# Placing the last two retention steps of each pair of heads with the planner margin that products have

## The chip, the cores and the metric

One Trainium2 chip, one of its cores. The metric is device microseconds (us) of one execution, median of the runs. The engines are TensorE (PE; its weight loads are shown apart as PEld), VectorE (DVE), ScalarE (ACT), GpSimd (POOL) and SyncE (SP, which here only issues DMAs).

## What is computed

One decoder layer over 1024 positions of width 1024, in float32. What matters here is the retention of four heads of 128, done chunk by chunk (8 chunks of 128 positions):

```
scores  = einsum('bhncd,bhnmd->bhncm', qc, kc) * intra_decay
o_intra = einsum('bhncm,bhnme->bhnce', scores, vc)
kv      = einsum('bhnmd,bhnme->nbhde', kc * zeta, vc)
state_n = chunk_decay * state_(n-1) + kv_(n-1)
o       = o_intra + einsum('bhncd,nbhde->bhnce', qc * xi, state)
y_ret   = group_rms_norm(o, ret_norm_g, 4 heads) * silu(rg)
```

Around it stand the other parts of the layer: `u = rms_norm(x)`, a combined projection `u @ w_in` of 3584 columns, a gated causal convolution of 512 channels with a norm of its own, the output projection `w_out`, a squared-ReLU MLP with 4096 hidden units and a last norm.

## The kernel before

**Precision and tiles.** Large products take each float32 operand as the sum of a rounded part and a rest and make three matmuls of 128x512 for each 128x128 block of weights (`mm`, line 403). A weight piece of 128x512 is split by ACT (`wh`, the rounded part) and DVE or POOL (`wl`, the rest), four pieces ahead of its use. Some products are formed in pairs by a seven-product scheme (`pair_in`, products 1, 2, 5, 6, 3, 7, 4) whose right-hand sides t1 to t4 are made by four tasks `rights(j)`, j = 0 to 3, from tiles `xs` loaded again from the input, and stored in tiles `U`.

**Order.** The program order of every engine is fixed when the kernel is built. In the mixer (the first 430 us or so) the large products are written out in a fixed order, and a planner puts the other work between them. The planner has a clock `now`, which advances by SLOT = 2.72 for each slot of 12 large matmuls, and a clock for ACT, DVE and POOL each, which advances by a cost for each instruction issued. For ACT the cost in us is 0.13 + 0.00095 for each column. After each slot `tick` lets the waiting tasks (Python generators) issue what is due. A task that yields an engine gets it when that engine can start within 3.2 us of `now`. A task that yields a number or nothing waits for that margin:

```
want = task.want
if want is None or isinstance(want, float):
    if task.ready + (want or PE_MARGIN) <= now[0] or look > 1e6:
        best = (-1.0, task, None)
        break
```

A task that yields a key waits until another has marked it. `force(key)` issues everything that is waiting, margins or not, until the key is marked. The margins are:

```
SLOT, LOOK, PE_MARGIN, LATE = 2.72, 3.2, 1.2, 0.0
NORM_MARGIN, STEP_MARGIN, POOL_LATE = 6.5, 0.3, 1.0
```

**Retention** (`retention(p, q, k)`, two heads for each p, called pair 0 and pair 1 below) is such a task of ten steps, c = 0 to 9, of which each adds 1.7 to `now`. A step c up to 7 makes the scores of chunk c. A step c from 1 to 8 makes the outputs of chunk c - 1 (lines 625 and 627, and 633 for the state) and normalises them: squares with row sums on ACT, then a chain of small operations on 128x2 numbers `m` (DVE, ACT, three times DVE), then the scaling of the 128x128 outputs on ACT into a tile `on` (tag `h`). A step c from 2 to 9 transposes the `on` of chunk c - 2 on the PE (line 663), and ACT copies the result into the head's tile `q`. So step 8 has four output matmuls and two transposes, and step 9 has two transposes. From step 7 on, the step sets its `ready` to the planner's clock of ACT as it stands after all of its ACT instructions. Step 8 marks ("retention", p). Pair 1 begins behind ("retention", 0), `rights(0)` and `rights(1)` wait for ("retention", 0), `rights(2)` and `rights(3)` for ("retention", 1), and `rights(1)` and `rights(3)` for the t4 of the one before. Step 9 marks the second half of the outputs ("o", h, 1); for heads 2 and 3 a task `put_by` then issues a store of 512 KB to DRAM on SP's queue (line 873), where weight loads (line 162) and loads of `xs` (line 793) are queued too.

Matmuls of pair 1's last steps lie among the products `whole(turn)` for the first five turns of IN_TURNS, at 158 to 233 us of the span; the first `pair_in` follows with the products 1 and 2, then product 5, which is the first to read a t1.

Of the kernel before, what the change touches and what calls it, by code (L numbers as in the profile page):

```python
# [23 lines left out]
NC_ = T // P  # L24
# [17 lines left out]
SLOT, LOOK, PE_MARGIN, LATE = 2.72, 3.2, 1.2, 0.0  # L42
WARM = 10
NORM_MARGIN, STEP_MARGIN, POOL_LATE = 6.5, 0.3, 1.0
# [35 lines left out]
def hybrid_layer(  # L80
# [498 lines left out]
    def retention(p, q, k):  # L579
# [5 lines left out]
        if p:  # L585
            yield "retention", 0
        for c in range(NC_ + 2):
            yield STEP_MARGIN
            now[0] += 1.7
            new = None  # L590
            if c < NC_:
# [165 lines left out]
    for p in range(2):  # L757
        q = rot_tiles(*ropes)
        if p == 0:
            rows_ = norm_rows()  # L760
        k = rot_tiles(*ropes)
        tick()
        spawn(retention(p, q, k), max(clock[dve], clock[pool]))
        retention_task[p] = procs[-1]
        del q, k
# [798 lines left out]
```

## Time and profile before

| what | value |
|---|---|
| median of 3 runs | 1071.01 us (1069.68 to 1071.92) |
| the profiled execution | 1070.03 us |
| its span, first to last instruction | 1068.1 us |
| PE busy | 1054.8 us of the span |
| DVE, ACT, POOL busy | 870.8, 463.6, 561.6 us |
| mean granted clock of TensorE | 0.999 |

The span is what the trace covers; the device time of that execution is 1.9 us longer. Matmuls overlap in the pipeline, so the start of one row to the start of the next is the time that a group takes, and the duration shown is longer. Times within rows are us from the start of the span.

### The profile page before, as it was taken

Reading aid. Unit: us, or ns where it says so; the run is one execution under the profiler, and the core shown is the slowest. Engines: PE = TensorE matmul, PEld = TensorE weight load, DVE = VectorE, ACT = ScalarE, POOL = GpSimd, SP = SyncE. Lnnn points to the kernel's source line nnn. Section 1 sums busy time; section 2 is a strip of 40 time slices with the busy share of each in tenths; the row PEclk is TensorE's granted clock in tenths of the full one; section 3 lists DMA queues with packets and bytes.
Section 4 is the critical chain, followed back from the end, with each engine's and each line's share of the span. In section 5 each row is a group of like instructions: output and inputs, shape, how many; then the busy total and the mean of one; then the engine's idle time right before and its main releaser. Section 6 shows DMA issues by size and latency. Waiting matters only on the chain.

```text
span 1068.1 us, 13853 instructions
## 1 busy us (share of the span) xinstructions
PE 1054.8 (99%) x4860; PEld 879.2 (82%) x4860; DVE 870.8 (82%) x1231; ACT 463.6 (43%) x906; POOL 561.6 (53%) x381
## 2 busy tenths in 40 slices
PE   9999999999999999999999999999999999999997
PEld 8888888788888888788788888888888888888886
DVE  7446546799998665799999989999899899899955
ACT  8211445673437444443343433343443434334453
POOL 6334324367854233559458267277186295384552
PEclk9999999999999999999999999999999999999999
DMA  7121122122223733051221211211301201200204
GB/s 276 65 58 42 38 80 70 63 95 80 69 69 129 256 115 123 11 187 39 61 59 49 79 31 50 90 30 50 99 21 50 89 21 49 90 21 19 69 30 158
DMA packets 39685, 82.25 MB, mean 77 GB/s; under 512 B 4544, under 2 KB 5696, under 8 KB 39616
## 3 DMA queue, kind: packets, MB, share of 16 engines
q1 hardware_dynamic: 39328, 80.85, 23.5%
q8 instruction: 38, 0.62, 0.2%
q10 hardware_dynamic: 288, 0.52, 0.1%
q14 instruction: 31, 0.25, 0.1%
HBM read 71.92 MB, written 9.44 MB: 76 GB/s over the span
## 4 chain that ended last, share of the span: by engine, by line
PE 90%; DVE 6%; ACT 2%; issue 1%; POOL 1%; DVEq 0%; ACTq 0%; POOLq 0%
PE b L403 55%; PE b L1277 23%; PE b L357 4%; PE b L1386 4%; DVE t L74 1%; DVE wl L74 1%; DVE x L74 1%; DVE m L74 1%; ACT h L74 1%; DVE q L74 1%; DVE V L74 1%; PE b L339 0%; PE b L595 0%; PE b L1436 0%; PE b L246 0%
## 5 line engine op out<-in xcount | busy, mean ns | idle before, releaser
L74 ACT CAST wh<-r 128x512 fp32r<-128x512 f32 x286 | 176.6, 620 | 326.4 <-PE b L403 134.4
L403 PE MATMUL b<-U,wh 128*128 128x512 f32 x1024 | 315.8, 390 | 2.0 <-DVE x L74 1.2
L74 DVE TENSOR_TENSOR wl<-r,wh 128x512 fp32r<-128x512 f32 x250 | 232.8, 933 | 89.0 <-ACT wh L74 87.8
L74 POOL TENSOR_TENSOR r<-r,r 128x512 f32<-128x512 f32 x136 | 210.2, 1548 | 114.1 <-DVE wl L74 66.1
L1277 PE MATMUL b<-V,wh 128*128 128x512 f32 x784 | 242.0, 389 | 0.7 <-POOL V L74 0.4
L403 PEld LDWEIGHTS b<-U,wh 128*128 128x128 f32 x1024 | 191.7, 188 | 43.2 <-issue 2.4
L74 DVE TENSOR_TENSOR x<-x,b 128x512 f32<-128x512 f32 (+1 forms) x312 | 195.5, 673 | 28.8 <-PE b L1386 14.3
L403 PE MATMUL b<-U,wl 128*128 128x512 f32 x512 | 199.2, 389 | 0.0
L1277 PEld LDWEIGHTS b<-V,wh 128*128 128x128 f32 x784 | 147.1, 188 | 32.4 <-POOL V L74 0.9
L74 POOL TENSOR_TENSOR t<-t,t 128x512 f32<-128x512 f32 x70 | 106.3, 1523 | 96.4 <-ACT t L74 50.4
L1277 PE MATMUL b<-V,wl 128*128 128x512 f32 x392 | 152.5, 389 | 0.0
L74 POOL TENSOR_TENSOR wl<-r,wh 128x512 fp32r<-128x512 f32 x36 | 51.4, 1432 | 119.3 <-ACT wh L74 116.5
L403 PEld LDWEIGHTS b<-U,wl 128*128 128x128 f32 x512 | 96.1, 188 | 19.9
L403 PE MATMUL b<-uh,wh 128*128 128x512 f32 x304 | 102.3, 396 | 0.0
L403 PE MATMUL b<-ul,wh 128*128 128x512 f32 x304 | 100.5, 390 | 0.0
L403 PE MATMUL b<-uh,wl 128*128 128x512 f32 x304 | 100.2, 389 | 0.0
L1277 PEld LDWEIGHTS b<-V,wl 128*128 128x128 f32 x392 | 73.6, 188 | 15.2
L74 POOL TENSOR_TENSOR V<-t,V 128x512 fp32r<-128x512 f32 x35 | 49.6, 1418 | 67.0 <-ACT V L74 67.0
L74 DVE TENSOR_TENSOR t<-t,b 128x512 f32<-128x512 f32 x112 | 75.8, 677 | 1.7 <-POOL t L74 1.2
L74 ACT ACTIVATE t<-t 128x512 f32<-128x512 f32 x64 | 40.2, 631 | 81.2 <-DVE t L74 80.5
L74 DVE TENSOR_TENSOR V<-t,V 128x512 fp32r<-128x512 f32 x63 | 70.3, 1116 | 0.0
L403 PEld LDWEIGHTS b<-uh,wl 128*128 128x128 f32 x304 | 57.0, 188 | 12.3
(177 smaller groups left out, 1431.3 us busy)
## 6 DMA issues: line engine op xcount, KB each, us to landing
r<-w_up_t SPq DMA_DIRECT2D x64, 256.0 KB, 2.6
r<-w_down_t SPq DMA_DIRECT2D x56, 256.0 KB, 2.7
r<-w_in_t SPq DMA_DIRECT2D x48, 256.0 KB, 2.7
xt<-xT SPq DMA_DIRECT2D x16, 256.0 KB, 5.4
xs<-xT SPq DMA_DIRECT2D x8, 512.0 KB, 5.0
r<-w_out_t SPq DMA_DIRECT2D x16, 256.0 KB, 2.7
x<-xT SPq DMA_DIRECT2D x8, 512.0 KB, 7.9
k<-x SPq DMA_DIRECT2D x6, 512.0 KB, 3.0
```

Of the source, the lines that this page charges most:

```text
L74: return f(out, *args, **kw)
L357: nc.tensor.matmul(vb[i], a[k][:, i * P : (i + 1) * P], b[k // 2][:, vs], start=(k == 0 and a is uh and b is vh), stop=(k == KT - 1 and a ...
L403: nc.tensor.matmul(b, a[:, k, :], rhs(n, k)[r], start=(start and i == 0), stop=(stop and i == len(ops) - 1),)
L1277: nc.tensor.matmul(b, a, r, start=(i == 0), stop=(i == len(ops) - 1))
L1386: nc.tensor.matmul(z, a, b, start=(k == 0 and t == 0), stop=(k == 3 and t == 2))
```

## The change

The steps 8 and 9 of each pair wait for 1.2 us in the planner behind their `ready`, as other tasks with a product in front of them do, instead of 0.3 us. Steps 0 to 7 keep 0.3. No instruction is added or taken away; the instructions of the two steps, and what the planner puts around them, can change place in the engines' program order.

```
@@ -585,7 +585,7 @@
         if p:
             yield "retention", 0
         for c in range(NC_ + 2):
-            yield STEP_MARGIN
+            yield STEP_MARGIN if c < NC_ else PE_MARGIN
             now[0] += 1.7
             new = None
             if c < NC_:
```

## Rows read from the trace of the kernel before

**Rows 1.** The page: the span, and the engines' busy time.

```profile
span 1068.1 us, 13853 instructions
PE 1054.8 (99%) x4860; PEld 879.2 (82%) x4860; DVE 870.8 (82%) x1231; ACT 463.6 (43%) x906; POOL 561.6 (53%) x381
```

**Rows 2.** Waits of PE, whole span: total us, times, longest.

```profile
PE b L663 <- ACT h L74: 2.3, 5, 0.7
```

**Rows 3.** Timeline of PE, pair 0's steps 8 and 9: start, us, [idle before].

```profile
146.83 0.38 PE L625 MATMUL b<-v,h 128*128 128x128 f32 x2
...
147.72 0.49 PE L663 MATMUL b<-ident,h 128*128 128x128 f32 x2
147.97 0.71 PE L403 MATMUL b<-uh,wh 128*128 128x512 f32 x2
...
150.82 0.38 PE L663 MATMUL b<-ident,h 128*128 128x128 f32 x2
150.96 0.71 PE L403 MATMUL b<-uh,wh 128*128 128x512 f32 x2
...
156.51 1.95 PE L339 MATMUL b<-ident,d 128*128 128x128 f32 x16
```

**Rows 4.** Timeline of PE, pair 1's steps 8 and 9.

```profile
204.82 0.38 PE L625 MATMUL b<-v,h 128*128 128x128 f32 x2
...
206.61 0.59 PE L663 MATMUL b<-ident,h 128*128 128x128 f32 x2 [0.73 <-ACT h L74]
206.95 0.71 PE L403 MATMUL b<-uh,wh 128*128 128x512 f32 x2
...
210.32 0.58 PE L663 MATMUL b<-ident,h 128*128 128x128 f32 x2 [0.35 <-ACT h L74]
210.66 0.71 PE L403 MATMUL b<-uh,wh 128*128 128x512 f32 x2
...
216.22 0.62 PE L403 MATMUL b<-uh,wh 128*128 128x512 f32 x2
```

**Rows 5.** Timeline of the other engines, pair 1's steps 7 and 8.

```profile
204.47 1.27 POOL L74 TENSOR_TENSOR xs<-xs 128x512 f32<-128x512 f32 x1
...
204.80 0.96 DVE L74 TENSOR_TENSOR m<-m 128x2 f32<-128x2 f32 x1 [0.27 <-ACT m L74]
...
207.53 0.31 ACT L74 ACTIVATE h<-b 128x128 f32<-128x128 f32 x1
...
207.73 1.30 POOL L74 TENSOR_TENSOR U<-xs,U 128x512 fp32r<-128x512 f32 x1 [1.99 <-ACT U L74]
...
208.21 0.83 DVE L74 SCALAR_TENSOR_TENSOR m<-m,bq 128x2 f32<-128x2 f32 x1 [0.61 <-ACT h L74]
...
209.90 0.62 ACT L74 ACTIVATE h<-b,m 128x128 f32<-128x128 f32 x2 [0.62 <-DVE m L74]
```

**Rows 6.** Timeline of ACT, pair 0's step 8: first square, scaling.

```profile
148.02 0.31 ACT L74 ACTIVATE h<-b 128x128 f32<-128x128 f32 x1
...
149.72 0.63 ACT L74 ACTIVATE h<-b,m 128x128 f32<-128x128 f32 x2 [0.62 <-DVE m L74]
```

**Rows 7.** Timeline of ACT, DVE and PE: the last scaling, t1 of rights(3), product 5.

```profile
226.30 2.18 ACT L74 ACTIVATE xs<-xs,sm 128x1024 f32<-128x1024 f32 x2
...
230.63 0.62 ACT L74 CAST U<-xs 128x512 fp32r<-128x512 f32 x1 [0.40 <-DVE xs L74]
...
234.28 0.68 DVE L74 TENSOR_TENSOR U<-xs,U 128x512 fp32r<-128x512 f32 x1
...
238.89 0.62 PE L403 MATMUL b<-U,wh 128*128 128x512 f32 x2
```

**Rows 8.** Timeline of SP's queue: stores of heads 2 and 3, loads behind them.

```profile
212.59 0.81 SPq L873 DMA_DIRECT2D sp<-q  x2
...
214.31 1.70 SPq L793 DMA_DIRECT2D xs<-xT  x2
```

**Rows 9.** Busy time by stretch: us, PE, PEld, DVE, ACT, POOL, PEclk, DMA share, GB/s.

```profile
211.00:233.40 22.40, 22.40 (x100) 18.54 (x99) 21.32 (x23) 17.03 (x29) 14.25 (x9) 1.00 0.29 106
...
350.00:380.00 30.00, 30.00 (x134) 24.86 (x133) 17.88 (x23) 13.63 (x24) 7.95 (x6) 1.00 0.56 204
```

More of the change, by code (lines that the diff above doesn't have):

```diff
@@ L587, in retention @@
         for c in range(NC_ + 2):
-            yield STEP_MARGIN
+            yield STEP_MARGIN if c < NC_ else PE_MARGIN
             now[0] += 1.7
```

## The prediction, made before the change was run

> **What bounds the kernel now.** I read the page first. PE is busy for 1054.8 of 1068.1 us [rows 1], so a change without arithmetic can only win back the 13.3 us in which PE stands. Next I read who made PE wait. The largest group is the transposes of the retention outputs, line 663, which waited for ACT's scaled tile `on` five times, 2.3 us in all [rows 2]. The change moves four of the ten transposing places, so I then read PE's timeline at these four. In pair 0 neither transpose is shown with a wait [rows 3]. In pair 1 both are: 0.73 us ahead of step 8's and 0.35 us ahead of step 9's [rows 4]. The other three waits lie at steps that the change leaves alone, and make 2.3 - 0.73 - 0.35 = 1.2 us. Last I read the other engines in pair 1 to see why `on` is late [rows 5], and what stands on the end of the two steps: `rights(2)` and `rights(3)`, and the stores [rows 7, 8].
>
> **Does the order change at all?** This follows from the code's own numbers. Step 7 and step 8 issue the same ACT work behind the start of their step: two squares, two scalings, two copies, each 0.13 + 0.00095 x 128 = 0.252, and one small root, 0.132. That is 1.64, so `ready` is at least 1.64 behind the step's `now`. The next `tick` comes 2.72 later. With the old margin 1.64 + 0.3 = 1.94 fits, with up to 0.78 of backlog on ACT to spare, and the rows show it: there is one slot of 12 matmuls between step 8 and step 9 in both pairs [rows 3, 4]. With the new one 1.64 + 1.2 = 2.84 never fits 2.72. So step 8 falls two slots behind step 7, and step 9 two behind step 8, as long as the backlog is under 5.44 - 2.84 = 2.60; for step 8 it is known to be at most 0.78. Step 8 goes one slot later, step 9 two slots later than before. No norm product, which would add 0.43 to `now`, stands between PE's large matmuls there up to the last of [rows 4].
>
> **What is won, place by place.** Starts of rows are used, since durations overlap.
> - Pair 0, step 8: the transposes take 0.49 against 0.38 at step 9 [rows 3], so 0.11 of hidden waiting. The whole step took 147.97 - 146.83 = 1.14, and 1.14 - 0.11 = 1.03 without it.
> - Pair 0, step 9: no wait, nothing won. It goes to the end of the last slot in front of the spreading of the norms at 156.51.
> - Pair 1, step 8: 206.95 - 204.82 = 2.13 [rows 4] against 1.03: 1.10.
> - Pair 1, step 9: from the matmul behind step 8 to the one behind step 9 it is 210.66 - 206.95 = 3.71 against 150.96 - 147.97 = 2.99 in pair 0: 0.72.
>
> Sum: 0.11 + 1.10 + 0.72 = 1.93 us. It exceeds the waits shown, since the matmuls behind a wait start unoverlapped. The slots cut by a step stay as many: PE executes the same instructions, with no added cost. I take the full 1.93, with 0 and 1.93 as the bounds of these three terms.
>
> **Do the waits come back at the new places?** Step 8's transposes need the `on` of chunk 6, which was there by 206.95 at the latest [rows 4]. The new step 8 begins one unbroken slot after 204.82. Two slots take 156.51 - 150.96 = 5.55, the first 150.82 - 147.97 = 2.85, so the second 2.70 [rows 3]: it begins at 207.52. No wait. It ends at 208.55, and step 9's transposes come 5.55 later, at 214.10. The `on` of chunk 7 must be there by then. The output matmuls of step 8 take 147.72 - 146.83 = 0.9 [rows 3], to 208.4. Before, ACT came to the squares at 207.53, 1.8 us after the matmuls (204.82 + 0.9); I take 0 to 1.8 again. From the first square to the end of the scaling it took 150.35 - 148.02 = 2.33 in pair 0 [rows 6], and 210.52 - 207.53 = 2.99 in pair 1 [rows 5]. So `on` is there between 210.7 and 213.2, at least 0.9 us early. In pair 0 step 9 gains two slots on an `on` that was in time.
>
> **What is late next.** Step 8 issues no DMA, but ("retention", 1) is marked one slot later, so `rights(2)` starts a slot, 2.72, later, and with it `rights(3)`. The first that PE needs of it is the t1 of `rights(3)`, in product 5. Its rest part ended on DVE at 234.96; product 5 starts at 238.89 [rows 7] and comes to the fourth of its blocks after 9 of 12 matmuls, at 238.89 + 9 x 2.72 / 12 = 240.93. Slack: 5.97. After, PE is there 1.93 earlier, and t1 may be 2.72 later: 5.97 - 1.93 - 2.72 = 1.3 us left. That hides it, at cost 0. DVE is busy for 21.32 of 22.40 us in that stretch [rows 9], so the slip may be more than one slot; this is the rival below. On SP's queue the two stores wait for step 9's copies and were issued at 212.59 [rows 8]. Step 9 goes from 210.32 to 214.10, so they go 3.8 later, and the loads of `xs` queued behind them may too, from 216.0 at the end of their issue to 219.8. The scaling that reads them began at 226.30 [rows 7]; 6.5 us remain for the transfer. Weight pieces are split four ahead, so a weight load a few us later is covered too. POOL has no instruction in either step; its share of `rights` moves with them and is counted above. From 350 us on DVE is busy 18 of 30 us [rows 9], so a backlog there is worked off and time won stays won.
>
> **Rivals.**
> - *The wait at step 9 stays, smaller.* In pair 1 the small `m` operations took 0.96 and 0.83 us, and each ended within 0.02 us of a POOL operation: 205.76 against 205.74, and 209.04 against 209.03 [rows 5]. One such hold lengthened the chain from 2.33 to 2.99. The chain has four such DVE operations. Two further holds of up to 0.8 would bring `on` to 213.2 + 1.6 = 214.8, 0.7 behind PE. Then some 0.7 to 0.9 of the 1.93 is lost: 1071.0 - 1.1 = 1069.9. It decides from the second further hold on. For it: POOL is 64% busy there [rows 9]. Against it: ACT's late start and both holds must fall together. The Trainium skill (SBUF — State Buffer, section "Who interferes with whom") states the reason: a DVE instruction with two SBUF inputs and a GpSimd instruction that reads SBUF exclude each other for a whole instruction. The two pairs of ends agree. By that rule the chain is exposed wherever POOL is busy, at the new place as well.
> - *Slower: t1 comes too late.* `rights` takes DVE, POOL or ACT some 30 times in `rights(2)` and `rights(3)`, and each may miss a slot. A slip of one slot leaves 1.3 us, two slots make PE wait 1.4, three 4.1. With the gain of 1.93 that is 1070.5 for two, and 1073.2 for three; it decides from the third slot on. For it: DVE has 1.1 us of idle time in 22.4. Against: one slot is what the planner gives, and tasks take the earliest engine.
> - *The gain is taken back.* DVE, 95% busy, is 1.93 us further behind PE from 211 us on, and PE waits for it once before 350: 1071.0. Against: PE waits for nothing in the 22.4 us behind the steps [rows 9].
> - *The change does nothing*, because a tick comes later than reckoned: 1071.0. The arithmetic above excludes it but for a `now` advanced by others.
> - *More is won*: the shifted order also frees a wait elsewhere, up to about 1 us: 1068.0.
>
> **Numbers.** The sum stands against the profiled execution: span 1068.1 - 1.93 = 1066.2, device 1070.03 - 1.93 = 1068.1. That execution is 0.98 under the median of the runs; against the median it is 1071.01 - 1.93 = 1069.08, 0.18% less. A difference of 0.2%, 2.14 us, is about what a measurement of this kernel can tell from none, so the forecast lies just inside. Chances: full gain 0.58, of which the runs' scatter puts some four in ten over 2.14; wait kept in part 0.15; taken back or nothing 0.10; late t1 0.11, of which 0.09 from three slots on; more won 0.06. Faster 0.24 + 0.06 = 0.30; slower 0.09; within 0.61. The range goes from the case "more won" with the scatter of the runs, about 1.1 either way, 1066.9, to the gain taken back with most of that scatter, 1071.9. It leaves out the late t1. The forecast's own range is 1068.0 to 1070.2.
>
> **What would show it.** In the trace after: two slots of 12 large matmuls on PE between steps 7 and 8 and between 8 and 9; waits of line 663 down from 2.3 in five to about 1.2 in three; step 8 of pair 1 at 207.4 to 207.5 and over in about 1.03; step 9 near 214.0; no new wait of PE at product 5, which comes near 237. The prediction is wrong if line 663 still waits at 214, if a row of line 403 reading `U` shows a wait, or if the first order differs before 204 us by more than pair 0's steps.

## The result, and the profile after

The change made the kernel slower: 1075.01 us, median of 5 runs (1074.42 to 1076.30), against 1071.01. The ratio on record is 1.0032, with a 95% interval from 1.0022 to 1.0043; the quotient of the two medians is 1.0037. The forecast of 1069.1 and its range up to 1071.9 both miss it. The profiled execution took 1074.43, and its span is 3.5 us longer than that of [rows 1]:

```profile
span 1071.6 us, 13853 instructions
...
PE 1055.2 (98%) x4860; PEld 879.6 (82%) x4860; DVE 868.6 (81%) x1230; ACT 463.0 (43%) x906; POOL 563.3 (53%) x382
```

PE did the same work (1055.2 us busy against 1054.8), so the added time is time in which it stood. The waits of PE over the whole span (engine, what waits, for what: us, times, longest) show a wait that [rows 2] does not have, at the top:

```profile
PE b L403 <- DVE z L74: 2.2, 1, 2.2
PE b L663 <- ACT h L74: 2.0, 4, 0.8
```

The order moved as forecast. This is PE's timeline after, for pair 0 and pair 1, to be read beside [rows 3, 4]:

```profile
149.76 0.38 PE L625 MATMUL b<-v,h 128*128 128x128 f32 x2
...
150.65 0.38 PE L663 MATMUL b<-ident,h 128*128 128x128 f32 x2
150.78 0.71 PE L403 MATMUL b<-uh,wh 128*128 128x512 f32 x2
...
156.36 0.38 PE L663 MATMUL b<-ident,h 128*128 128x128 f32 x2
...
207.62 0.38 PE L625 MATMUL b<-v,h 128*128 128x128 f32 x2
...
208.51 0.38 PE L663 MATMUL b<-ident,h 128*128 128x128 f32 x2
208.65 0.71 PE L403 MATMUL b<-uh,wh 128*128 128x512 f32 x2
...
215.17 0.59 PE L663 MATMUL b<-ident,h 128*128 128x128 f32 x2 [0.79 <-ACT h L74]
215.51 0.71 PE L403 MATMUL b<-uh,wh 128*128 128x512 f32 x2
```

Step 8 of pair 1 is where it should be (207.62) and its transposes no longer wait: the whole step takes 208.65 - 207.62 = 1.03. But step 9's transposes, two slots later, wait 0.79, more than the 0.35 of [rows 4]. The `on` of chunk 7, expected between 210.7 and 213.2, was scaled from 214.75 on. Why it is late stands in the timeline of ACT, DVE and POOL between the two steps, the rows that answer to [rows 5]:

```profile
209.16 0.30 ACT L74 ACTIVATE h<-b 128x128 f32<-128x128 f32 x1
...
209.58 0.23 ACT L74 ACTIVATION_READ_ACCUMULATOR h<-b 128x1 f32 x1
213.04 0.20 ACT L74 ACTIVATE m<-m 128x2 f32<-128x2 f32 x1 [3.23 <-DVE m L74]
214.75 0.62 ACT L74 ACTIVATE h<-b,m 128x128 f32<-128x128 f32 x2 [1.51 <-DVE m L74]
...
206.14 3.89 DVE L74 SCALAR_TENSOR_TENSOR cv<-a,sm,cv 128x511 f32<-128x511 f32 x4
209.95 1.78 DVE L74 TENSOR_TENSOR wl<-r,wh 128x512 fp32r<-128x512 f32 x1
211.66 1.28 DVE L74 TENSOR_TENSOR z<-b,R 128x512 f32<-128x512 f32 x2
212.85 0.15 DVE L74 SCALAR_TENSOR_TENSOR m<-m,bq 128x2 f32<-128x2 f32 x1
213.28 1.05 DVE L74 TENSOR_TENSOR m<-m 128x2 f32<-128x2 f32 x1 [0.27 <-ACT m L74]
...
213.01 1.29 POOL L74 TENSOR_TENSOR z<-z,cv 128x512 f32<-128x512 f32 x1
```

Read them in this order. ACT squares at 209.16 and has the row sums at 209.81 (209.58 + 0.23). Its next instruction in program order is the small root, which needs DVE's `m`. DVE's `m` now stands in DVE's program order behind four `cv`, one `wl` and two readings of product banks, which run without a gap until 212.9. Before, it stood behind the first two of the four `cv`. So ACT, which executes in order too, stands for 3.23 us, and 1.51 more until the chain is through; the second `m` operation takes 1.05 us and ends at 214.33, beside the POOL operation that ends at 214.30. Together ACT did almost nothing for 5 us.

POOL also stretches the work in front of the chain. It runs without a gap from 207.81 to 212.89, and two operations of DVE's queue take long beside it. One is the fourth `cv`:

```profile
208.37 1.67 DVE L74 SCALAR_TENSOR_TENSOR cv<-a,sm,cv 128x512 f32<-128x512 f32 x1
...
207.81 1.68 POOL L74 TENSOR_TENSOR U<-xs,U 128x512 fp32r<-128x512 f32 x1 [2.00 <-ACT U L74]
...
209.45 1.74 POOL L74 TENSOR_TENSOR U<-xs,U 128x512 fp32r<-128x512 f32 x1
```

The four `cv` together took 3.89, so the other three took some 0.74 each. The other is the `wl`, with 1.78; in the kernel before, a `wl` at 221.29, while POOL stood idle, took 0.68. Both end some 0.55 us behind the end of a POOL operation: 210.04 behind 209.49, and 211.73 behind 211.19. So they took some 0.9 and 1.1 us longer, and the second `m` operation another 0.9 (1.05 against 0.16 before): 2.9 us in all, each beside a POOL operation.

That starves DVE next. These are its waits between 205 and 265 us after (before, DVE waited for none of `U`, `xs` and `s` in that stretch):

```profile
DVE U L74 <- ACT U L74: 2.5, 4, 0.9
DVE xs L74 <- ACT xs L74: 1.6, 2, 1.2
...
DVE s L74 <- ACT s L74: 1.0, 2, 0.5
```

and the busy time by stretch, which answers to [rows 9]: DVE was busy for 16.89 of the 22.40 us, where it had been busy for 21.32.

```profile
211.00:233.40 22.40, 21.61 (x96) 17.47 (x96) 16.89 (x25) 16.33 (x31) 13.37 (x10) 1.00 0.30 106
```

PE does not notice at once. It comes to product 5 at 238.31, 0.58 earlier than in [rows 7], with no wait, but only just: the rest part of the t1 of `rights(3)` ends at 239.60 + 0.69 = 240.29, and PE comes to the block that reads it at 240.35:

```profile
239.60 0.69 DVE L74 TENSOR_TENSOR U<-xs,U 128x512 fp32r<-128x512 f32 x1 [0.35 <-ACT U L74]
...
240.35 0.62 PE L403 MATMUL b<-U,wh 128*128 128x512 f32 x2
```

It notices at the first whole product behind the last pair, which needs a PSUM bank (a buffer that takes a product's results until another engine has read them) that the third of three DVE readings `z<-z,b` releases. Timelines of DVE and PE there, first before, then after:

```profile
309.07 2.19 DVE L74 TENSOR_TENSOR z<-z,b 128x512 f32<-128x512 f32 x3
...
311.43 0.62 PE L403 MATMUL b<-uh,wh 128*128 128x512 f32 x2
```

```profile
311.63 2.19 DVE L74 TENSOR_TENSOR z<-z,b 128x512 f32<-128x512 f32 x3
...
311.34 0.39 PE L403 MATMUL b<-uh,wh 128*128 128x512 f32 x1
313.88 0.50 PE L403 MATMUL b<-uh,wh 128*128 128x512 f32 x1 [2.15 <-DVE z L74]
```

Before, the bank was free at 309.07 + 2.19 = 311.26 and PE's second matmul used it at 311.43 + 0.23 = 311.66: 0.4 us to spare. After, DVE comes 2.56 later, and PE waits 2.15. At this place the kernel is 313.88 - 311.66 = 2.2 us behind. The rest of the 3.5 us came up behind 436 us, where the largest wait that the two profiles do not share is 0.70 us and comes and goes with one and the same kernel (before_again below).

### The profile page after: what moved, and what is told of

Same layout as the page of the kernel before. It is cut to its first block, busy times and chain, and to the rows that moved or that the text cites. A ratio compares the mean times of both kernels' runs of the same rounds, so it can differ in the third digit from the quotient of the medians.

```text
span 1071.6 us, 13853 instructions
## 1 busy us (share of the span) xinstructions
PE 1055.2 (98%) x4860; PEld 879.6 (82%) x4860; DVE 868.6 (81%) x1230; ACT 463.0 (43%) x906; POOL 563.3 (53%) x382
## 4 chain that ended last, share of the span: by engine, by line
PE 82%; DVE 9%; POOL 3%; issue 3%; ACT 2%; DMA 1%; DVEq 0%; POOLq 0%; ACTq 0%
PE b L403 48%; PE b L1277 22%; PE b L357 4%; PE b L1386 4%; DVE wl L74 2%; DVE z L74 1%; DVE cv L74 1%; DVE t L74 1%; POOL r L74 1%; DVE x L74 1%; DVE m L74 1%; DMA x<-k 1%; POOL x L74 1%; ACT h L74 1%; DVE q L74 1%
```

## The experiments

Two theories. **A:** DVE's new place for the `m` chain holds ACT, ACT starves DVE, and DVE's lateness makes PE wait at 312. **B:** ("retention", 1) is marked a slot later, so the `rights` tasks start late and crowd DVE at the wrong time; the hold matters little. Ratios are to the kernel before, with 95% intervals; its median lay between 1070.95 and 1071.48 in these comparisons.

### Which pair, which step

**pair0** and **pair1** give the new margin to one pair alone:

```
-            yield STEP_MARGIN
+            yield PE_MARGIN if c >= NC_ and p == 0 else STEP_MARGIN
```

(pair1: `p == 1`.)

> Only pair 0's steps 8 and 9 get the new margin. Theory A (pair 1's step 8 does the harm: its DVE chain stands behind other DVE work and holds ACT): nothing of the loss is here, the time is 0.1 us under before, 1070.9, within 0.5. Theory D (pair 0's later steps shift the planner's clocks and so everything behind): about +4 us, 1075.

> Only pair 1's steps 8 and 9 get the new margin. Theory A and theory B (the tasks rights(2) and rights(3) start a slot later): the whole loss, about 1075, PE waits some 2.1 us for DVE near 314 us. Theory D: 1071.

Measured: pair0 1071.51, 0.9999 (0.9990 to 1.0009); pair1 1076.34, 1.0045 (1.0029 to 1.0062). The loss is all in pair 1, where PE again waits 0.83 at step 9 and 2.16 for `z`.

**last9** and **last8** move one step of pair 1 alone (`c > NC_ and p == 1`, and `c == NC_ and p == 1`).

> Only step 9 of pair 1 gets the new margin, step 8 stays. Theory A: no harm, since step 8's chain stands where it was; step 9's wait (0.72) goes, but DVE comes to the product at 311 us with only 0.4 us to spare, so of the 0.72 some 0.3 is left: 1070.3 to 1071.2. Theory C (the later step 9, its stores and the outputs it marks, does the harm): 1073 or more.

> The kernel before with only the second-last step of heads 2 and 3 moved one slot later; the last step follows it one slot behind, as before. VectorE's program order around the step is that of pair1, TensorE's has the last step one slot earlier. Theory A (VectorE's place in its own program order sets the time, and TensorE only arrives at it): the last step's transposes wait for the scaled tile until about 215, some 3 us instead of 0.83, but the lateness further on is VectorE's and stays that of pair1: 1074.5 to 1077, with a wait under 1 us left at the product near 312. Rival (the waits of TensorE add up): 1076.3 + 2.3 = 1078.6, with the 2.2 us wait near 312 still there.

last9: 1073.96, 1.0025 (1.0016 to 1.0034). Theory A's number was missed by 3 us, and the time is what theory C gave: a later step 9 alone, with step 8 and the mark in their old places, costs some 2.7 us. Step 9 no longer waits and step 8 waits 0.76, much as in [rows 4]. But the planner, whose clocks have moved, puts the `rights` operations on DVE, ACT and POOL in another order from 212 us on, and PE waits for DVE at product 5 (the place that the prediction had feared) and at the bank. No wait for the stores or for the outputs, which C named, is seen:

```profile
242.57 0.50 PE L403 MATMUL b<-U,wh 128*128 128x512 f32 x1 [1.64 <-DVE U L74]
...
314.77 0.50 PE L403 MATMUL b<-uh,wh 128*128 128x512 f32 x1 [1.37 <-DVE z L74]
```

last8: 1076.08, 1.0042 (1.0027 to 1.0057). Its DVE has the program order of pair1 around the step, but PE comes to step 9 a slot earlier:

```profile
214.95 0.73 PE L663 MATMUL b<-ident,h 128*128 128x128 f32 x2 [3.50 <-ACT h L74]
215.33 1.20 PE L403 MATMUL b<-uh,wh 128*128 128x512 f32 x2
...
315.64 0.62 PE L403 MATMUL b<-uh,wh 128*128 128x512 f32 x2
```

The wait at step 9 is 3.50 instead of 0.83, the one at the bank is gone (A had expected up to 1 us of it), and the time is that of pair1, as A expected and not the rival: the waits do not add up. DVE starts the three readings at 313.00, 0.69 later than in pair1 (312.31) and 3.9 later than before, so it is late at either place where PE meets it. How TensorE's clock enters stands at the end.

### The hold of ACT

**actroot** is the kernel after, in which step 8 of pair 1 makes the root with two small ACT instructions instead of the DVE chain; the refinement of the root is left out for chunk 7 of heads 2 and 3. The planner's clocks are charged as before, and PE's order is that of after.

```
+                if p == 1 and c == NC_:
...
+                    for j in range(2):
+                        nc.scalar.activation(
+                            m2[:, 0, j : j + 1], m[:, j : j + 1], AF.Abs_reciprocal_sqrt,
+                            bias=by_query[:, h0 + j, pc : pc + 1], scale=1.0 / P,
+                        )
```

**actroot_before** is the same replacement in the kernel before, as a control.

> The changed kernel, but in step 8 of pair 1 the four small DVE operations of the normalisation are left out and the root is taken by two small ACT instructions (the one refinement of that root is left out for heads 2 and 3 of chunk 7). PE's order is that of the changed kernel to the last instruction, the planner's clocks too. Theory A: ACT is not held for 4.7 us, step 9's wait of 0.79 goes, DVE is not 2.6 us late, the wait of 2.15 us near 314 shrinks to under 1.5 (PE then comes earlier than before, DVE as before): 1070.0 to 1071.3. Theory B: 1075 less the 1.0 of step 9's wait at most, 1074 or more, since the tasks start as late as in the changed kernel.

> Control for actroot: the same replacement of the root for chunk 7 of heads 2 and 3 (two ScalarE operations for four small VectorE ones, the refinement of the root left out) in the kernel before, whose steps stand where they stood. Theory A (the gain of actroot over after came from lifting the hold of ScalarE that the moved step made): here there is little hold to lift, only the 0.35 us wait at the last step, so 1070.3 to 1071.5. Rival (four fewer small VectorE operations are worth some 3 us by themselves, wherever the step stands): about 1068.

actroot: 1071.80, 1.0005 (0.9996 to 1.0015), 3.2 us under after, though 0.5 over A's range. actroot_before: 1071.36, 1.0000 (0.9990 to 1.0009). So the removed operations are worth nothing that can be told where they stood, and 3.2 us where the change put them. ACT's and PE's timelines of actroot (its profiled execution, 1074.16, is the slowest of its ten):

```profile
209.93 0.50 ACT L657 ACTIVATE m<-m,bq 128x1 f32<-128x1 f32 x2
210.31 0.65 ACT L74 ACTIVATE h<-b,m 128x128 f32<-128x128 f32 x2
...
309.96 0.39 PE L403 MATMUL b<-uh,wh 128*128 128x512 f32 x1
312.14 0.50 PE L403 MATMUL b<-uh,wh 128*128 128x512 f32 x1 [1.79 <-DVE z L74]
```

ACT scales at 210.31 instead of 214.75, and step 9 does not wait. Yet the time is that of before and not under it. PE starts the product at 309.96, 1.47 ahead of before's 311.43, and waits 1.79 at the bank (A had under 1.5) for a DVE that is no earlier than it was: it starts the three readings at 309.90, before at 309.07. The forecast's gain was won here and taken back 100 us later.

### The mark

**markearly** is after with the mark one step earlier for pair 1, where it stood in time before; **marklate** is before with the mark one step later:

```
-            if c == NC_:
+            if c == NC_ - p:
```

(marklate: `NC_ + p`.)

> The changed kernel, with the key on which rights(2) and rights(3) wait marked by step 7 of pair 1 in place of step 8, so these tasks start no later than before. Step 8's DVE chain still stands behind four conv operations, a weight rest and two bank readings. Theory A: ACT is held for about 4.7 us as in the changed kernel, and the time stays high, 1073 to 1076. Theory B (the tasks' late start is the cause): 1070 to 1071.

> The kernel before, with that key marked by step 9 of pair 1 in place of step 8: the tasks start one slot later, the steps stay. Theory A: ACT is not held, 1071 within 1. Theory B: 1074 to 1075.

markearly: 1072.26, 1.0011 (1.0002 to 1.0020), between what A and B gave. ACT is held nearly as long as in after (3.42 + 0.62 us against 3.23 + 1.51), but has scaled the first `xs` of `rights(2)` by then (at 208.34, in after at 218.49), and DVE is busy for 20.82 us in the stretch of [rows 9]. PE still waits 1.75 at the bank. marklate: 1073.49, 1.0017 (1.0007 to 1.0027), also between the two, with a wait at a product behind product 5 and none at the bank:

```profile
246.56 0.50 PE L403 MATMUL b<-U,wh 128*128 128x512 f32 x1 [1.48 <-POOL U L74]
```

So B is right in part: a late mark by itself costs some 2 us, and an early one mends most of the loss. That the hold hurts because the work behind it starts late as well fits this, but is not shown. A and B are not two amounts to be added: each of actroot and markearly, which mend one of the two, brings back about 3 of 4 us. DVE's start of the three readings at the bank tells somewhat more: 311.63 in after, 310.76 in markearly, 309.90 in actroot, and 309.07 and 310.02 in the two profiles of before. Lifting the hold brings back more of DVE's lateness than the early mark, though two profiles of one kernel differ by nearly as much.

### The bank at 312

**lag** is before with 13 idle copies of 128x128 on DVE at the start of the pair (6, 7). **swap_after**, **swap_before** and **swap_actroot** change which of two rings of banks the last pair's products take in turn, so that the whole product behind it takes another one; no engine's order changes:

```
-            b = product(n, (pm, pr)[at % 2])
+            b = product(n, ((pr, pm) if fs == (10, 11) else (pm, pr))[at % 2])
```

**before_again** is the kernel before, unchanged, in one profiled execution.

> The kernel before with 13 DVE copies of 128x128 (into the mask's tile, which nothing reads any more) in front of the second pair of products, at about 252 us, unknown to the planner; all else in the same order. It adds L us of DVE time, to be read from the trace, estimated 1.5 to 2.6. If DVE has only the 0.4 us to spare at the product near 311 that the trace of before shows, PE waits L - 0.4 there, and the time is 1071 + L - 0.4. If DVE's lag is worked off on the way (the rival: the wait near 314 in the changed kernel has another cause), no wait and 1071.

> The changed kernel with the two groups of PSUM banks exchanged in the last pair of products alone, so that the product at 311 to 314 us gets banks that DVE has emptied several us earlier; the order of every engine stays. Theory A: the wait of 2.15 us goes, and since PE had come there 0.2 us ahead of the kernel before, the time is that of before, 1071.3 within 0.6. If DVE's lag is met again at the next bank, 1073 or more.

> The kernel before with the same exchange of banks. Its product at 311 us does not wait, so nothing is won: 1071.3 within 0.6, by both theories.

> The run without DVE operations in step 8's chain (the refinement of that root is left out for heads 2 and 3 of chunk 7), with the same exchange of banks. If the gain of some 1.9 us at steps 8 and 9 is there and was only taken back by the wait of 1.79 us at 312, the time is 1.7 under before: 1069.6 within 0.6. If the gain was never there, 1071 or more.

> The kernel before once more, for its profile: whether the wait of 0.7 us of PE for a DVE result near 500 us, which the profiles of the changed kernel and of the run with pair 0 alone show and the first profile of before does not, comes and goes without any change. If so it is seen here, or the stretch from 436 us to the end is again 631.8; if it is of the change, never here.

lag: 1075.54, 1.0041 (1.0027 to 1.0056). The copies in DVE's timeline, and PE at the bank:

```profile
258.66 5.96 DVE L829 COPY causal<-R 128x128 f32<-128x128 f32 x13
...
315.61 0.50 PE L403 MATMUL b<-uh,wh 128*128 128x512 f32 x1 [2.11 <-DVE z L74]
```

The copies took 5.96 us where 1.5 to 2.6 were estimated. DVE works off part of that: at the bank it starts the three readings at 313.36, 3.3 later than in before_again. The rest is not worked off. Besides a wait of 0.59 for a late `wl` it comes out as the wait that after has, in a kernel whose retention is untouched. So the expected wait, L - 0.4, comes out too large, and the rival, which had none, fails.

swap_before: 1071.19, 1.0001 (0.9992 to 1.0010), so the swap is worth nothing by itself. swap_after: 1072.65, 1.0014 (1.0005 to 1.0023); PE has no wait at the bank any more, and its waits from 230 to 480 us are

```profile
PE b L403 <- DVE x L74: 1.1, 2, 0.7
PE b L484 <- POOL s L74: 0.6, 1, 0.6
PE b L403 <- DVE wl L74: 0.2, 1, 0.2
```

of which only the first stands in before too. So the bank's wait carries 1075.01 - 1072.65 = 2.4 us. It lies 1.35 us over the middle of what was expected; the 0.6 and 0.2 us are new waits for a late POOL and DVE, which would make some 0.8 of it. Of the rest some 0.6 lies outside the span: the median span of its executions is 1070.0 us, 1.1 over the 1068.9 of before's, where the device times differ by 1.70. swap_actroot, without hold and without the bank's wait (and with the same refinement left out): 1070.23, 0.9994 (0.9985 to 1.0003), just over the expected range, and the interval does not tell it from before. In its profile PE starts the product at 309.62 without a wait behind it, 1.81 ahead of before's 311.43, where the forecast had 1.93. So the local gain is there at 312, but of it the median shows only 0.7 us, which is not clear of noise. In the profile a part goes to later waits, such as 0.26 us for POOL's `s` at 323.87.

before_again: 1071.28. Its PE shows a wait that the other profile of the same kernel does not have, and that after has as well, with 0.70 at 500.45:

```profile
498.47 0.70 PE L403 MATMUL b<-U,wh 128*128 128x512 f32 x2 [0.39 <-DVE t L74]
```

## Why the prediction was wrong

- **The order, and step 8: right.** Two slots in front of each step, step 8 of pair 1 at 207.62 (forecast 207.52) without a wait, over in 1.03. Pair 0's step 9 lost nothing by its move (pair0: 0.9999).
- **The sum of what is won: right in size.** With the hold lifted and the bank swapped, PE is 1.81 ahead at 312 (swap_actroot), against 1.93. One count in the reading is wrong without harm: the transposing places are sixteen (steps 2 to 9 of two pairs), not ten.
- **"Do the waits come back at the new places?": this step failed.** It took the chain from square to scaling over from before, 2.33 to 2.99 us, and added ACT's lateness alone. From 209.16 to 214.75 + 0.62 = 215.37 it took 6.2. The chain's duration belongs to the place in the program order, not to the chain: DVE had other work from 206.14 to 212.85, 6.7 us, in front of its first link, and the row sums, ready at 209.81, waited 3.0 us for it. From the matmul behind step 8 to the one behind step 9 PE took 215.51 - 208.65 = 6.86, where two slots and the transposes take 5.55 + 0.14 [rows 3]: 1.17 lost. 1.93 - 1.17 leaves 0.76; at product 5 PE is 0.58 earlier, or 0.68 counted from the transposes that start at 197.00 before and 197.10 after.
- **The rival of the smaller wait: right in kind, wrong in size.** A hold by POOL did come, on the second `m` operation (1.05 us, ending with POOL's at 214.3), as the rule of the Trainium skill has it (SBUF — State Buffer, "Who interferes with whom"). In the chain it is some 0.9 of the delay. The queue in front of the chain is the larger part, and the prediction did not look at it; but of the 3.0 us by which the queue came late, some 2.0 are POOL's too, at the fourth `cv` and the `wl`. Without the three, and if nothing else had come late, `on` would have been there at about 215.37 - 2.9 = 212.5 (an estimate), in front of the 214.10 of the forecast. The rival counted holds in the chain alone; the loss at step 9, 0.7 to 0.9 there, was 1.17.
- **"What is late next": right where it looked, in part by luck, and it looked at the wrong place.** t1 was in time, but by 0.06 us where 1.3 was reckoned: its rest part ended 240.29 - 234.96 = 5.33 later, nearly two slots and not one, and PE came only 0.58 earlier (5.97 - 0.58 - 5.33 = 0.06). With the full gain of 1.93 PE would have waited 1.3 there. The stores and the loads behind them went late without harm: SP issued the stores at 220.34, 7.8 later than in [rows 8] where 3.8 was reckoned, and the scaling that reads `xs` began at 229.13 instead of 226.30 and waited for no transfer. But the mark a slot later, costed at 0, costs some 2 us alone (marklate), and "time won stays won" was argued from the idle DVE behind 350 us, while DVE is busy for 88 to 97% all the way to the bank at 311, where 0.4 us was left. That slack could have been read from the trace of before.
- **The rival "taken back" had the right place in kind** (a PE wait for DVE before 350) but reckoned with a DVE that stays where it was. Then the kernel would have ended at before's time, as actroot does. In after DVE itself is 2.56 late, so the sign turned.
- **The size.** At the bank the profile shows 2.2 us. In some executions the clock, below, adds 1.5. How the loss splits between the hold and the late mark stays open: mending either brings back most of it. Nor are these two the only ways to it: last9 has neither, and loses 2.7 us with the `rights` operations in another order. In all three PE ends up waiting for work of DVE or POOL behind the steps: at product 5, at one behind it, or at the bank. The last us or so between profile and median is within what single executions differ by.

## What to carry to other kernels

Before a step is moved in a statically ordered program, write down what will stand in front of each of its instructions on every in-order engine, not only on the engine that waited; a chain of tiny operations that hops between two busy engines costs what is queued ahead of each hop, and holds both. Before time is called won, follow the busiest helper engine (here DVE, at 95% of the stretch behind the steps) up to the next place where the bound engine needs something from it, and read the slack there, however far off it is. A wait that disappears while the helper's end stays put reappears at that place, as actroot shows.

## What the runs showed of the hardware

A wait of PE can cost a second time, through the clock. After its 3.50 us wait, last8's matmuls ran at a granted clock of 0.50, the lower level of 1.2 GHz, from 215 to 219 us; busy time by stretch (the column with 1.00 and 0.50 is the granted clock):

```profile
205.00:211.00 6.00, 6.00 (x33) 5.14 (x32) 5.86 (x8) 3.55 (x12) 4.01 (x4) 1.00 0.61 220
...
215.00:217.00 2.00, 2.00 (x6) 1.63 (x7) 0.79 (x2) 1.97 (x6) 0.00 (x0) 0.50 0.04 8
217.00:219.00 2.00, 2.00 (x6) 1.52 (x6) 0.97 (x2) 1.97 (x6) 0.00 (x0) 0.50 0.41 162
...
221.00:225.00 4.00, 4.00 (x20) 3.30 (x19) 3.93 (x5) 1.43 (x3) 1.29 (x1) 1.00 0.88 336
```

Twelve matmuls took 220.44 - 215.33 = 5.11 us there, against 211.50 - 208.65 = 2.85 at full clock in after. That is 2.3 us on top of the wait, so last8 and pair1 end together in part because the fall came at another wait. Behind the waits of about 2 us at the bank it fell in some executions only. In pair1's profile it did:

```profile
314.56 0.50 PE L403 MATMUL b<-uh,wh 128*128 128x512 f32 x1 [2.16 <-DVE z L74]
...
319.21 0.61 PE L403 MATMUL b<-ul,wh 128*128 128x512 f32 x2
```

These 13 matmuls from 314.56 to 319.21 take 4.65 us, and 3.12 in the profile of after (313.88 to 317.00), where the clock stayed at 1.00 behind a wait of the same length. Of the five runs of after, two have a mean clock of 0.998 and spans of 1071.6 and 1072.4, and three have 0.996 or 0.997 and spans of 1073.1 to 1073.8: so the median of 1075.01 seems to contain such a fall, though only one of the five is seen in a trace.
